# Handing 384 columns of the last row to GpSimd and ScalarE, with the row's pieces cut anew, in a transfer-bound loss kernel

## Chip, cores, metric

One core of a Trainium2 chip. The metric is the device time of one execution in microseconds (us), as the median of several runs. The span in a profile, from the first instruction to the last, is some 1.4 us shorter than the time (82.5 against 83.9).

Row b of a partition is called "row b" below: each of the 128 partitions holds 8 rows of 4096 columns, and a "column" is one fp32 in every partition. VectorE is DVE in the profile, ScalarE is ACT, GpSimd is POOL, SyncE is SP. SBUF and PSUM are the two memories in which the kernel keeps its tiles. A load has landed when its data is there; the releaser of a wait is what ended it.

## The reference

```python
batch, dim = 1024, 4096            # log_input, target: fp32, 16.8 MB each
loss = np.exp(log_input) - target * log_input
return np.mean(loss, axis=-1)      # one number per row
```

## The kernel before

SyncE issues all loads. ScalarE sums exp(x) of a row with its accumulator; VectorE multiplies target by log_input, negated, and sums with its own; a small ScalarE activation joins the two partial sums of a row. The tiles hold six of the eight rows, so rows 6 and 7 go into the space of rows 0 and 3. The last row is loaded in pieces, so that little is left to do once the last piece has landed. Its partial sums stand in columns behind row 3's space of the target tile, against columns of -1 in the log_input tile, so that VectorE's last multiply adds them up as well.

```python
TAIL = [("x", 100), ("t", 52), ("t", 48), ("x", 28), ("t", 14), ("t", 14)]   # last row, in 32 columns
...
loads += [("x", 0, d), ("x", d, 3 * d), ("t", 0, 4 * d)]
for first, rows in ((4, 2), (6, 1)):
    loads += [("x", first * d, rows * d), ("t", first * d, rows * d)]
at = {"x": last_row * d, "t": last_row * d}
for what, w in TAIL:
    loads.append((what, at[what], w * d // 128))
...
    nc.scalar.activation(out=e_dump[:, col : col + w], in_=place("x", lo, w),    # e_dump: PSUM
        func=ACT_F.Exp, bias=0.0, scale=1.0, accum_out=...)
...
    nc.vector.tensor_tensor_reduce(out=place("t", lo, w), in0=place("t", lo, w),
        in1=place("x", lo, w), scale=-1.0, op0=ALU.mult, op1=ALU.add, accum_out=...)
...
    # the last piece: w + n_parts columns, waits for the landing, the last exp
    # and the last-but-one multiply through one semaphore
```

Of the kernel before, what the change touches and what calls it, by code (L numbers as in the profile page):

```python
# [5 lines left out]
ACT_F = mybir.ActivationFunctionType  # L6
ALU = mybir.AluOpType
F32 = mybir.dt.float32


TAIL = [("x", 100), ("t", 52), ("t", 48), ("x", 28), ("t", 14), ("t", 14)]


def before_first_barrier(nc, instructions):





    here, first = nc.cur_bb.bb, nc.main_func.blocks[0]  # L20
    names = {i.name for i in instructions}
    here.instructions = [i for i in here.instructions if i.name not in names]
    at = next(
        k
        for k, i in enumerate(first.instructions)
        if i.engine == mybir.EngineType.SP and i.opcode == "Drain"
    )
    first.instructions = first.instructions[:at] + instructions + first.instructions[at:]


def kernel(tc, log_input, target, out):















    nc = tc.nc
    tc.close()
    tc.compile()  # L49

    P = nc.NUM_PARTITIONS
    n, d = log_input.shape
    nb = n // P
    assert nb * P == n and tuple(target.shape) == (n, d) and nb == 8 and d % 128 == 0
    inv_d = 1.0 / d
    last_row = nb - 1

    x_v = log_input.rearrange("(p b) d -> p (b d)", b=nb)
    t_v = target.rearrange("(p b) d -> p (b d)", b=nb)
    out_v = out.rearrange("(p b) -> p b", b=nb)  # L60


    loads = []
# [6 lines that stand above are left out]
        at[what] += w * d // 128  # L70
    assert at == {"x": nb * d, "t": nb * d}


    def work(kind):
        todo = []
        for i, (what, lo, w) in enumerate(loads):
            if what == kind:
                step = min(w, d)
                todo += [(a, step, i) for a in range(lo, lo + w, step)]
        return todo  # L80

    x_work, t_work = work("x"), work("t")
    n_x, n_t = len(x_work), len(t_work)
    n_parts = n_x - last_row + n_t - last_row - 1

    big = {
        "x": nc.alloc_sbuf_tensor("x_big", [P, 4 * d + n_parts], F32).ap(),
        "t": nc.alloc_sbuf_tensor("t_big", [P, 4 * d + n_parts], F32).ap(),
    }
    mid = {  # L90
        "x": nc.alloc_sbuf_tensor("x_mid", [P, 2 * d], F32).ap(),
        "t": nc.alloc_sbuf_tensor("t_mid", [P, 2 * d], F32).ap(),
    }

    def place(what, lo, w):
        row = lo // d
        if 4 <= row < 6:
            return mid[what][:, lo - 4 * d : lo - 4 * d + w]
        if row >= 6:
            lo -= (6 if row == 6 else 4) * d  # L100
        return big[what][:, lo : lo + w]

    e_dump = nc.alloc_psum_tensor("e_dump", [P, d], F32).ap()

    parts = nc.alloc_sbuf_tensor("parts", [P, 2 * last_row], F32).ap()
    join_dump = nc.alloc_sbuf_tensor("join_dump", [P, 2 * last_row], F32).ap()
    all_loss = nc.alloc_sbuf_tensor("all_loss", [P, nb], F32).ap()

    def part(k):
        return big["t"][:, 4 * d + k : 4 * d + k + 1]  # L110

    landed = [nc.alloc_semaphore(f"landed{i}") for i in range(len(loads) - 1)]


    last_ready = nc.alloc_semaphore("last_ready")
    exp_done = nc.alloc_semaphore("exp_done")
    prod_done = nc.alloc_semaphore("prod_done")
    join_done = nc.alloc_semaphore("join_done")
    ones_done = nc.alloc_semaphore("ones_done")
    loss_done = nc.alloc_semaphore("loss_done")  # L120
    out_done = nc.alloc_semaphore("out_done")


    early = []
    for i, (what, lo, w) in enumerate(loads):
        if what == "x" and lo in (6 * d, 7 * d):
            free = 1 if lo == 6 * d else 4
            nc.sync.wait_ge(exp_done, free)
            nc.sync.wait_ge(prod_done, free)  # L129
        src = x_v if what == "x" else t_v  # L130
        dma = nc.sync.dma_start(out=place(what, lo, w), in_=src[:, lo : lo + w])  # L131
        dma.then_inc(landed[i] if i < len(loads) - 1 else last_ready, 16)
        if lo < 6 * d:
            early.append(dma.ins)
    before_first_barrier(nc, early)


    nc.gpsimd.memset(big["x"][:, 4 * d : 4 * d + n_parts], -1.0).then_inc(ones_done, 1)  # L138


    def join(row, exps):
        nc.scalar.wait_ge(exp_done, exps)
        nc.scalar.activation(  # L143
            out=join_dump[:, 2 * row : 2 * row + 2],
            in_=parts[:, 2 * row : 2 * row + 2],
            func=ACT_F.Copy,
            scale=inv_d,
            accum_out=all_loss[:, row : row + 1],
        ).wait_op(prod_done, row + 1, "sem-ge").then_inc(join_done, 1)

    for k, (lo, w, i) in enumerate(x_work):
        row, col = lo // d, lo % d
        if col == 0 and row >= 2:
            join(row - 2, k)
        elif col == 0 and row == 1:
            nc.scalar.wait_ge(exp_done, k)
        nc.scalar.activation(  # L157
            out=e_dump[:, col : col + w],
            in_=place("x", lo, w),
            func=ACT_F.Exp,  # L160
            bias=0.0,
            scale=1.0,
            accum_out=parts[:, 2 * row : 2 * row + 1] if row < last_row else part(k - last_row),
        ).wait_op(landed[i], 16, "sem-ge").then_inc(
            exp_done if k < n_x - 1 else last_ready, 1
        )
        if col == 0 and row == last_row:
            join(row - 1, k + 1)


    waited = set()
    for j, (lo, w, i) in enumerate(t_work):
        row = lo // d
        x_load = next(ix for a, wx, ix in x_work if a + wx >= lo + w)
        if x_load not in waited:
            nc.vector.wait_ge(landed[x_load], 16)
            waited.add(x_load)
        if j < n_t - 1:
            nc.vector.tensor_tensor_reduce(  # L179
                out=place("t", lo, w),  # L180
                in0=place("t", lo, w),
                in1=place("x", lo, w),
                scale=-1.0,
                scalar=0.0,
                op0=ALU.mult,
                op1=ALU.add,
                accum_out=parts[:, 2 * row + 1 : 2 * row + 2]
                if row < last_row
                else part(n_x - last_row + j - last_row),
            ).wait_op(landed[i], 16, "sem-ge").then_inc(  # L190
                prod_done if j < n_t - 2 else last_ready, 1
            )
        else:
            nc.vector.wait_ge(ones_done, 1)
            nc.vector.wait_ge(exp_done, n_x - 1)
            nc.vector.wait_ge(prod_done, n_t - 2)  # L196
            nc.vector.tensor_tensor_reduce(  # L197
                out=place("t", lo, w + n_parts),
                in0=place("t", lo, w + n_parts),
                in1=place("x", lo, w + n_parts),  # L200
                scale=-inv_d,
                scalar=0.0,
                op0=ALU.mult,
                op1=ALU.add,
                accum_out=all_loss[:, last_row : last_row + 1],
            ).wait_op(last_ready, 18, "sem-ge").then_inc(loss_done, 1)


    nc.sync.wait_ge(join_done, last_row)
    nc.sync.dma_start(out=out_v, in_=all_loss).wait_op(loss_done, 1, "sem-ge").then_inc(  # L210
        out_done, 16
    )
    used = landed + [last_ready, exp_done, prod_done, join_done, ones_done, loss_done]
    nc.sync.sem_clear(range(used[0].num, out_done.num))
    assert all(used[0].num <= s.num < out_done.num for s in used)
    nc.sync.wait_ge(out_done, 16).then_inc(out_done, -16)
# [30 lines left out]
```

## Time and profile before

| | before |
|---|---|
| median of the first three runs | 83.94 us (83.93 to 84.05) |
| bytes loaded | 33.55 MB |
| mean transfer rate over the span | 407 GB/s |
| busy: VectorE / ScalarE / GpSimd | 35.6 / 32.9 / 0.3 us |
| last multiply | 453 columns, 0.63 us |

The engines' busy shares (43%, 40%, 0%) are averages over a long stretch of waiting for data and a short crowded tail. The kernel is bound by its loads (the packets of the load queue took 95.8% of the 16 DMA engines' span, by the page), and what can be changed by compute is only what hangs over their end.

### The profile page before, as it was taken

What the parts mean: (1) busy time and instruction counts of PE and PEld (TensorE: products, weight loads), DVE (VectorE), ACT (ScalarE), POOL (GpSimd) and SP (SyncE); (2) the same over time, 40 slices, a digit from 0 to 9 for tenths busy, and PEclk for the clock granted to TensorE, in tenths of its full rate; (3) what the DMA queues carried; (4) which work ended last, traced back from release to release, by engine and by line L of the source; (5) the groups of instructions that cost most, each with busy time, mean ns of one, the idle gap of its engine ahead of it and who ended that gap; (6) DMA issues with size and microseconds to landing.
All of it is one profiled execution on the core that took longest, in us unless ns stands there. A gap on an engine that the chain in (4) does not pass through costs nothing.

```text
span 82.5 us, 130 instructions
## 1 busy us (share of the span) xinstructions
DVE 35.6 (43%) x22; ACT 32.9 (40%) x33; POOL 0.3 (0%) x5
## 2 busy tenths in 40 slices
DVE  0000000000000000000199999999369995993992
ACT  0325920000592000000000998979792496009450
POOL 0000000000000000000000000000000000000000
DMA  5998998888999990999599799599798999999960
GB/s 127 421 469 381 620 524 381 381 381 381 509 509 509 509 509 0 509 509 509 254 509 445 318 509 509 254 509 509 310 453 381 461 429 410 441 383 420 402 234 2
DMA packets 2017, 33.56 MB, mean 407 GB/s; under 512 B 353, under 2 KB 609, under 8 KB 993
## 3 DMA queue, kind: packets, MB, share of 16 engines
q1 hardware_dynamic: 2016, 33.56, 95.8%
q14 instruction: 1, 0.00, 0.0%
HBM read 33.55 MB, written 0.00 MB: 407 GB/s over the span
## 4 chain that ended last, share of the span: by engine, by line
DMA 69%; DVE 17%; issue 11%; SPq 1%; DVEq 0%
DMA t_big<-in_target_dram 69%; DVE t_big L179 16%; SPq L131 1%; DVE t_big L197 1%; DVE parts L179 0%; DVEq L196 0%; SPq L129 0%; DVE all_loss L197 0%
## 5 line engine op out<-in xcount | busy, mean ns | idle before, releaser
L179 DVE CUSTOM_DVE_ANT_0 t_big<-t_big,x_big 128x4096 f32<-128x4096 f32 (+3 forms) x8 | 26.1, 3298 | 43.4 <-DMA t_big<-in_target_dram 43.4
L157 ACT ACTIVATE e_dump<-x_big 128x4096 f32<-128x4096 f32 (+2 forms) x7 | 21.7, 3095 | 19.6 <-DMA x_big<-in_log_input_dram 19.4
L143 ACT ACTIVATE join_dump<-parts 128x2 f32<-128x2 f32 x7 | 1.4, 203 | 24.3 <-DVE parts L179 24.2
L179 DVE CUSTOM_DVE_ANT_0 t_mid<-t_mid,x_mid 128x4096 f32<-128x4096 f32 x2 | 8.8, 4422 | 2.0 <-DMA t_mid<-in_target_dram 2.0
L157 ACT ACTIVATE e_dump<-x_mid 128x4096 f32<-128x4096 f32 x2 | 7.1, 3568 | 0.0
L157 ACT ACT_TABLE_LOAD x1 | 1.3, 1283 | 3.4 <-PEq L49 3.4
L143 ACT ACTIVATION_READ_ACCUMULATOR join_dump<-parts 128x1 f32 x7 | 1.3, 187 | 0.0
L157 ACT ACTIVATION_READ_ACCUMULATOR e_dump<-x_big 128x1 f32 x7 | 1.3, 186 | 0.0
L197 DVE CUSTOM_DVE_ANT_0 t_big<-t_big,x_big 128x453 f32<-128x453 f32 x1 | 0.6, 631 | 0.0
L179 DVE DVE_READ_ACCUMULATOR2_ANT parts<- 128x1 f32 x7 | 0.6, 81 | 0.0
L157 ACT ACTIVATION_READ_ACCUMULATOR e_dump<-x_mid 128x1 f32 x2 | 0.4, 186 | 0.0
L179 DVE DVE_READ_ACCUMULATOR2_ANT t_big<- 128x1 f32 x3 | 0.2, 81 | 0.0
L138 POOL MEMSET x_big<- 128x5 f32 x1 | 0.1, 103 | 3.0 <-POOLq L49 3.0
L231 POOL MEMSET const-bfloat16-1.0<- 128x1 bf16 x1 | 0.1, 102 | 0.0
L231 POOL MEMSET const-uint8-127<- 128x1 uint8 x1 | 0.1, 102 | 0.0
L231 POOL MEMSET const-float32-0.0<- 128x1 f32 x1 | 0.1, 98 | 0.2 <-issue 0.2
L231 POOL MEMSET const-float32-1.0<- 128x1 f32 x1 | 0.1, 98 | 0.0
L197 DVE DVE_READ_ACCUMULATOR2_ANT all_loss<- 128x1 f32 x1 | 0.1, 81 | 0.0
## 6 DMA issues: line engine op xcount, KB each, us to landing
x_big<-in_log_input_dram SPq DMA_DIRECT2D x1, 6144.0 KB, 21.2
x_big<-in_log_input_dram SPq DMA_DIRECT2D x2, 2048.0 KB, 13.4
x_mid<-in_log_input_dram SPq DMA_DIRECT2D x1, 4096.0 KB, 49.3
t_mid<-in_target_dram SPq DMA_DIRECT2D x1, 4096.0 KB, 58.5
t_big<-in_target_dram SPq DMA_DIRECT2D x1, 2048.0 KB, 24.3
x_big<-in_log_input_dram SPq DMA_DIRECT2D x1, 1600.0 KB, 15.5
t_big<-in_target_dram SPq DMA_DIRECT2D x1, 832.0 KB, 17.1
t_big<-in_target_dram SPq DMA_DIRECT2D x1, 768.0 KB, 18.5
```

The lines of the kernel that those rows point to most:

```text
L131: dma = nc.sync.dma_start(out=place(what, lo, w), in_=src[:, lo : lo + w])
L138: nc.gpsimd.memset(big["x"][:, 4 * d : 4 * d + n_parts], -1.0).then_inc(ones_done, 1)
L143: nc.scalar.activation(out=join_dump[:, 2 * row : 2 * row + 2], in_=parts[:, 2 * row : 2 * row + 2], func=ACT_F.Copy, scale=inv_d, accum_o ...
L157: nc.scalar.activation(out=e_dump[:, col : col + w], in_=place("x", lo, w), func=ACT_F.Exp, bias=0.0, scale=1.0, accum_out=parts[:, 2 * ro ...
L179: nc.vector.tensor_tensor_reduce(out=place("t", lo, w), in0=place("t", lo, w), in1=place("x", lo, w), scale=-1.0, scalar=0.0, op0=ALU.mult ...
L197: nc.vector.tensor_tensor_reduce(out=place("t", lo, w + n_parts), in0=place("t", lo, w + n_parts), in1=place("x", lo, w + n_parts), scale= ...
L231: nc = _bacc.Bacc("TRN2", target_bir_lowering=False, num_devices=1)
```

## The change

Its intent is to take work off VectorE near the end. GpSimd multiplies 384 of the first piece's 2560 columns and ScalarE sums those products. So that VectorE and GpSimd do not get in each other's way in SBUF, ScalarE first copies the other 2176 columns of log_input to PSUM, and VectorE reads them there. The exps of the last row go to an unused part of SBUF, so that they do not write where VectorE reads. The pieces are cut anew.

```diff
-TAIL = [("x", 100), ("t", 52), ("t", 48), ("x", 28), ("t", 14), ("t", 14)]
+TAIL = [("x", 80), ("t", 80), ("x", 30), ("t", 30), ("x", 18), ("t", 8), ("t", 10)]
+SHARE = 12
...
+    gp_x = place("x", shared_lo + dve_w, gp_w)
+    gp_t = place("t", shared_lo + dve_w, gp_w)
+    nc.gpsimd.wait_ge(landed[x_work[last_row][2]], 16)
+    nc.gpsimd.tensor_tensor(out=gp_t, in0=gp_t, in1=gp_x, op=ALU.mult).wait_op(
+        landed[shared_load], 16, "sem-ge").then_inc(gp_done, 1)
...
+        if k == last_row:
+            nc.scalar.activation(
+                out=e_dump[:, :dve_w], in_=place("x", lo, dve_w), func=ACT_F.Copy
+            ).wait_op(landed[i], 16, "sem-ge").then_inc(copy_done, 1)
+        if k == last_row + 1:
+            nc.scalar.activation(out=dump[:, :gp_w], in_=gp_t, func=ACT_F.Copy,
+                scale=-1.0, accum_out=part(n_parts - 1),
+            ).wait_op(gp_done, 1, "sem-ge").then_inc(sum_done, 1)
...
+        x_cols = place("x", lo, w)
+        if j == last_row:
+            w = dve_w
+            x_cols = e_dump[:, :w]
+            nc.vector.wait_ge(copy_done, 1)
...
-                in1=place("x", lo, w),
+                in1=x_cols,
```

(Cut: the semaphores, the place of the exps' output, and one more partial sum.)

More of the change, by code (lines that the diff above doesn't have):

```diff
@@ L83 @@
     n_x, n_t = len(x_work), len(t_work)
-    n_parts = n_x - last_row + n_t - last_row - 1
+    n_parts = n_x - last_row + n_t - last_row
+    shared_lo, shared_w, shared_load = t_work[last_row]
+    gp_w = SHARE * d // 128
+    dve_w = shared_w - gp_w
+    assert shared_lo == x_work[last_row][0] and shared_w <= x_work[last_row][1]
     big = {
@@ L118 @@
     join_done = nc.alloc_semaphore("join_done")
+    copy_done = nc.alloc_semaphore("copy_done")
+    gp_done = nc.alloc_semaphore("gp_done")
+    sum_done = nc.alloc_semaphore("sum_done")
     ones_done = nc.alloc_semaphore("ones_done")
@@ L138 @@
     nc.gpsimd.memset(big["x"][:, 4 * d : 4 * d + n_parts], -1.0).then_inc(ones_done, 1)
+    gp_x = place("x", shared_lo + dve_w, gp_w)
+    gp_t = place("t", shared_lo + dve_w, gp_w)
+    nc.gpsimd.wait_ge(landed[x_work[last_row][2]], 16)
+    nc.gpsimd.tensor_tensor(out=gp_t, in0=gp_t, in1=gp_x, op=ALU.mult).wait_op(
+        landed[shared_load], 16, "sem-ge"
+    ).then_inc(gp_done, 1)
     def join(row, exps):
@@ L149, in join @@
         ).wait_op(prod_done, row + 1, "sem-ge").then_inc(join_done, 1)
+    dump = big["x"][:, d : 2 * d]
     for k, (lo, w, i) in enumerate(x_work):
@@ L156 @@
             nc.scalar.wait_ge(exp_done, k)
+        if k == last_row:
[3 more added lines that the diff above has]
+        if k == last_row + 1:
+            nc.scalar.activation(
+                out=dump[:, :gp_w],
+                in_=gp_t,
+                func=ACT_F.Copy,
+                scale=-1.0,
+                accum_out=part(n_parts - 1),
+            ).wait_op(gp_done, 1, "sem-ge").then_inc(sum_done, 1)
         nc.scalar.activation(
-            out=e_dump[:, col : col + w],
+            out=e_dump[:, col : col + w] if row < last_row else dump[:, col : col + w],
             in_=place("x", lo, w),
@@ L194 @@
             nc.vector.wait_ge(ones_done, 1)
+            nc.vector.wait_ge(sum_done, 1)
             nc.vector.wait_ge(exp_done, n_x - 1)
@@ L212 @@
     )
-    used = landed + [last_ready, exp_done, prod_done, join_done, ones_done, loss_done]
+    used = landed + [last_ready, exp_done, prod_done, join_done, copy_done, gp_done]
+    used += [sum_done, ones_done, loss_done]
     nc.sync.sem_clear(range(used[0].num, out_done.num))
```

## The prediction

(Cut from the prediction: what a PSUM operand costs VectorE, what a column costs GpSimd, who of the two is held, and rival (d), that GpSimd's first multiply comes late. The sum came to -0.04 us, so 83.9 us. Its terms stand, but the last start at 80.45 (the +0.09) holds the cut term for the PSUM operand; without that term the start is the 80.39 of rival (a), and the 0.15 us of slack that ScalarE has up to it shrinks with it. That a PSUM operand speaks against rivals (b) and (c) was not shown then. That GpSimd keeps ahead of ScalarE, and the 85.6 and 84.8 of rivals (b) and (c), rest on a length of its multiply that is cut.)

> **What bounds the kernel now.** I read the page's DMA row first, then the chain of waits, then the timeline of the last microseconds, then the landing times of the single loads.
>
> ```profile
> span 82.5 us, 130 instructions
> ...
> DVE  0000000000000000000199999999369995993992
> ACT  0325920000592000000000998979792496009450
> POOL 0000000000000000000000000000000000000000
> DMA  5998998888999990999599799599798999999960
> ```
>
> The DMA row is at nine tenths in most slices up to the last two. VectorE idles for 41 us, since target arrives late. So the inputs (33.55 MB) set the time, and compute matters only where it hangs over the end of the transfers. The change leaves rows 0 to 6 alone, as the list of instructions per engine confirms. Only the tail can move.
>
> The chain that ended last, in order of time:
>
> ```profile
> 58.92 17.14 DMA t_big<-in_target_dram
> 76.05 0.02 issue
> 76.08 3.05 DVE t_big L179 x3
> ...
> 80.25 0.09 DVE t_big L179
> 80.34 0.02 issue
> 80.36 0.63 DVE t_big L197
> 81.00 0.01 DVE all_loss L197
> ```
>
> From 76.05 on it is no longer a DMA but VectorE that the chain runs through: it works through its backlog of target pieces. The timeline of that stretch:
>
> ```profile
> 74.04 2.84 ACT L157 ACTIVATE e_dump<-x_big 128x3200 f32<-128x3200 f32 x1 [4.51 <-DMA x_big<-in_log_input_dram]
> 76.08 1.89 DVE L179 CUSTOM_DVE_ANT_0 t_big<-t_big,x_big 128x1664 f32<-128x1664 f32 x1 [1.44 <-DMA t_big<-in_target_dram]
> 77.96 1.76 DVE L179 CUSTOM_DVE_ANT_0 t_big<-t_big,x_big 128x1536 f32<-128x1536 f32 x1
> 79.10 0.92 ACT L157 ACTIVATE e_dump<-x_big 128x896 f32<-128x896 f32 x1 [1.72 <-DMA x_big<-in_log_input_dram]
> 79.70 0.62 DVE L179 CUSTOM_DVE_ANT_0 t_big<-t_big,x_big 128x448 f32<-128x448 f32 x1
> 80.36 0.63 DVE L197 CUSTOM_DVE_ANT_0 t_big<-t_big,x_big 128x453 f32<-128x453 f32 x1
> 81.03 0.35 SPq L210 DMA_DIRECT2D out_dram<-all_loss  x1
> ```
>
> The view of one line's DMA issues gives each load's time from issue to landing. Issue start plus that time: log_input's 3200 columns land at 58.55 + 15.5 = 74.05, its 896 at 59.88 + 19.2 = 79.08, target's last two pieces at 60.36 + 19.3 = 79.66 and 60.86 + 19.4 = 80.26; row 6 of target landed at 45.88 + 24.3 = 70.18. So the last piece of data is there at 80.26 and the last multiply starts at 80.36. VectorE's backlog over the transfers is therefore only 0.1 us. What lies behind the last landing is 0.1 of backlog, 0.63 for the last multiply, 0.03, and 1.4 for the output's transfer. Only the first two, about 0.7 us of 83.94, are in reach of this change.
>
> [...]
>
> **Working scales, from rows of the trace.** VectorE: 4422 ns for 4096 columns and 624 for 448 give 1.041 ns a column plus 158 ns. ScalarE exp: 3580 for 4096 and 922 for 896 give 0.831 ns a column plus 178; an accumulator read starts 0.05 to 0.07 before an activation's end, takes 0.19, and the next ScalarE instruction starts 0.09 after the read starts. Transfers: 3200 columns in 74.05 - 70.18 = 3.87 us and 448 in 0.59 give 1.19 ns a column and about 0.05 us for each load.
>
> **The change part by part.**
> *Loads.* The same 8192 columns in seven loads in place of six: 0.05 us more. Working forward from 70.18: log_input 2560 at 73.3, target 2560 at 76.4, log_input 960 at 77.6, target 960 at 78.8, log_input 576 at 79.5, target 256 at 79.9, target 320 at 80.3. All issues stand ready by about 61.5 (six of them are over at 61.3 now, each some 0.45 us), long before the data, so the extra issue is hidden.
>
> *VectorE.* Its first piece now has 2560 - 384 = 2176 columns: 2.42 us from 76.4[...]: free at 78.85 or so. The 960 columns landed at 78.8: 1.16 us, to 80.0. The 256 columns landed at 79.9: 0.42, to 80.42. The last one can start at about 80.45, in place of 80.36. It has 320 + 7 = 327 columns in place of 453: 0.50 in place of 0.63. End at 80.95 against 80.99: a gain of 0.04. Without giving 384 columns away, the same sizes would put VectorE 384 x 1.041 = 0.40 us later[...]. In both kernels VectorE waits for the last row's first target piece; that one now lands 0.3 us later (76.4 against 76.06) and leaves 384 columns less to do, so the two nearly cancel.
>
> *ScalarE.* It was idle from 69.5 to 74.04, and now has a copy and a sum more. Copy of 2176: 73.3 to 75.2 (1.81 + 0.1), ahead of the target's landing at 76.4, so it costs VectorE no wait. Exp 2560: 75.2, its accumulator read at 77.45 to 77.65. Join of row 6: 77.74, next instruction at 77.94. Sum of the 384 products: 77.94 to 78.46 for the next start. Exp 960: 78.46, next at 79.46. Exp 576: landed 79.5, accumulator read out at 80.3. That is just ahead of VectorE's 80.45, and 0.15 us is all its slack.
>
> *GpSimd.* Multiply of 384 columns from 76.4[...]. ScalarE asks for it at 77.94[...].
>
> *Sum.* Transfers +0.05, which VectorE's lag covers; VectorE's last start +0.09; last multiply -0.13. Total -0.04 us, with an uncertainty of 0.1 from all these small terms. I choose 83.9 us, which is level.
>
> **The rivals.**
> (a) *Everything fits and VectorE has no backlog.* If the PSUM read costs nothing extra, the last start is at 80.39, set by VectorE, or 80.31 by the last landing, and the gain is 0.1 to 0.17: 83.8. Nothing could give more, as the last 320 columns can't start before they land.[...]
> (b) *GpSimd becomes the wait.* If the multiply is held until VectorE's 2176 columns are through, at 78.85[...]; sum, exp 960 and exp 576 follow on ScalarE, 0.52 + 1.0 + 0.85 later, so that the last multiply starts at 82.2: 1.8 later, minus 0.13, 85.6 us, at the edge of 2%.[...] A slower multiply, of 2.5 us say, would give 84.7.
> (c) *VectorE is held by GpSimd*[...]: 84.8.[...]
> [...]
>
> **Range and chances.** The main case and (a) hold 83.75 to 84.0 and carry about four fifths. A small slip of ScalarE or GpSimd (some tenths) makes up most of the rest, up to 84.5. (b), (c) and (d) carry about a tenth, of which some 5 points are over 2%. A gain of 2% (1.68 us) is out of reach: less than 0.8 us lies behind the last landing ahead of the output. So 83.9, from 83.7 to 84.5; faster 0.01, within 2% 0.94, slower 0.05.
>
> **What the profile after would show.** Right: target's last landing at 80.2 to 80.4; the 2176-column piece at 2.4 to 2.5 us, starting with its landing at 76.4; the GpSimd multiply starting there too and over before 78, with no idle time of ScalarE ahead of its sum; the last VectorE piece at 0.50 us from 80.3 to 80.5. Wrong: ScalarE idle with GpSimd named as releaser (b); the 2176-column piece at over 3 us (c)[...]. The prediction fails if the GpSimd multiply takes over 2 us, or if the added instructions move something ahead of 70 us.

## The result

The changed kernel takes 83.98 us (83.77 to 84.14, 6 runs), the one before 83.97 us (83.82 to 84.05, 6 runs). Ratios here and below are those from the runs of both kernels in the same rounds; they are not quite the ratio of the medians quoted. Here the ratio is 1.0001, with a 95% interval of 0.9982 to 1.002: the same.

The page of the changed kernel, busy tenths in 40 slices (each about 2.06 us), for the two engines that gained work, and DMA:

```profile
span 82.5 us, 141 instructions
ACT  0324930000493000000000998979792496049990
POOL 0000000000000000000000000000000000000400
DMA  6999998888999982999599899699699999999960
```

ScalarE, half idle before in the last four slices (9450), is now full there (9990). GpSimd has one visible stretch. DMA is as full as before, to the same slice.

The chain of waits of the changed kernel, in order of time (start, length, what; "issue" is time in which the profile shows no wait):

```profile
59.05 17.43 DMA t_big<-in_target_dram
76.48 0.02 issue
76.50 1.23 DVE t_big L222
77.73 1.12 issue
78.85 0.86 DVE t_big L222 x2
...
80.50 0.02 issue
80.53 0.50 DVE t_big L241
```

It is the same chain: transfers, then VectorE's pieces up to the last multiply. Neither GpSimd nor ScalarE is in it. The timeline of its tail (start, length, engine, line, operation; in brackets idle time and what ended it):

```profile
70.32 4.43 DVE L222 CUSTOM_DVE_ANT_0 t_big<-t_big,x_big 128x4096 f32<-128x4096 f32 x1 [1.00 <-DMA t_big<-in_target_dram]
73.41 1.99 ACT L184 ACTIVATE e_dump<-x_big 128x2176 f32<-128x2176 f32 x1 [3.76 <-DMA x_big<-in_log_input_dram]
76.50 2.42 DVE L222 CUSTOM_DVE_ANT_0 t_big<-t_big,e_dump 128x2176 f32<-128x2176 f32 x1 [1.75 <-DMA t_big<-in_target_dram]
76.55 1.00 POOL L160 TENSOR_TENSOR t_big<-t_big,x_big 128x384 f32<-128x384 f32 x1 [73.00 <-DMA t_big<-in_target_dram]
78.04 0.51 ACT L188 ACTIVATE x_big<-t_big 128x384 f32<-128x384 f32 x1
78.85 0.08 DVE L222 DVE_READ_ACCUMULATOR2_ANT t_big<- 128x1 f32 x1
78.92 1.16 DVE L222 CUSTOM_DVE_ANT_0 t_big<-t_big,x_big 128x960 f32<-128x960 f32 x1
79.68 0.68 ACT L195 ACTIVATE x_big<-x_big 128x576 f32<-128x576 f32 x1
80.00 0.08 DVE L222 DVE_READ_ACCUMULATOR2_ANT t_big<- 128x1 f32 x1
80.06 0.43 DVE L222 CUSTOM_DVE_ANT_0 t_big<-t_big,x_big 128x256 f32<-128x256 f32 x1
80.53 0.50 DVE L241 CUSTOM_DVE_ANT_0 t_big<-t_big,x_big 128x327 f32<-128x327 f32 x1
```

GpSimd's multiply is over at 77.55, before ScalarE asks for it at 78.04. The last piece was issued at about 61.5 and took 18.9 to land, so it was there at 80.4; the last multiply began 0.1 later, just as before.

**A measure that the scatter of the runs does not blur.** Runs of one kernel differ by 0.2 to 0.4 us (83.82 to 84.05 and 83.77 to 84.14 above). Part of that is when the stream of loads reaches row 7, which neither kernel changes (row 6's multiply starts at 70.21 and 70.43 in two traces of the kernel before). So for every trace I take the *tail*: from the start of VectorE's row 6 piece, which starts with the landing of row 6, to the end of the last multiply. Before it is 80.36 + 0.63 - 70.21 = 10.78 us; in the changed kernel 80.53 + 0.50 - 70.32 = 10.71.

### The profile page after: what moved, and what is told of

It is laid out like the page before. It is cut to its first block, busy times and chain, and to the rows that moved or that the text cites. A ratio compares the mean times of both kernels' runs of the same rounds, so it can differ in the third digit from the quotient of the medians.

```text
span 82.5 us, 141 instructions
## 1 busy us (share of the span) xinstructions
DVE 35.2 (43%) x22; ACT 35.5 (43%) x38; POOL 1.3 (2%) x6
## 4 chain that ended last, share of the span: by engine, by line
DMA 70%; DVE 15%; issue 12%; SPq 1%; DVEq 0%
DMA t_big<-in_target_dram 70%; DVE t_big L222 15%; SPq L147 1%; DVE t_big L241 1%; DVE parts L222 0%; DVEq L240 0%; SPq L145 0%; DVE all_loss L241 0%
## 5 line engine op out<-in xcount | busy, mean ns | idle before, releaser
L222 DVE CUSTOM_DVE_ANT_0 t_big<-t_big,x_big 128x4096 f32<-128x4096 f32 (+2 forms) x7 | 23.5, 3386 | 42.1 <-DMA t_big<-in_target_dram 42.1
L195 ACT ACTIVATE e_dump<-x_big 128x4096 f32<-128x4096 f32 x5 | 17.9, 3580 | 13.4 <-DMA x_big<-in_log_input_dram 13.3
L195 ACT ACTIVATE x_big<-x_big 128x2560 f32<-128x2560 f32 (+2 forms) x3 | 4.0, 1330 | 0.1
L184 ACT ACTIVATE e_dump<-x_big 128x2176 f32<-128x2176 f32 x1 | 2.0, 1988 | 3.8 <-DMA x_big<-in_log_input_dram 3.8
L222 DVE CUSTOM_DVE_ANT_0 t_big<-t_big,e_dump 128x2176 f32<-128x2176 f32 x1 | 2.4, 2421 | 1.7 <-DMA t_big<-in_target_dram 1.7
L160 POOL TENSOR_TENSOR t_big<-t_big,x_big 128x384 f32<-128x384 f32 x1 | 1.0, 1000 | 73.0 <-DMA t_big<-in_target_dram 73.0
L195 ACT ACTIVATION_READ_ACCUMULATOR x_big<-x_big 128x1 f32 x3 | 0.6, 186 | 0.0
L241 DVE CUSTOM_DVE_ANT_0 t_big<-t_big,x_big 128x327 f32<-128x327 f32 x1 | 0.5, 499 | 0.0
L188 ACT ACTIVATE x_big<-t_big 128x384 f32<-128x384 f32 x1 | 0.5, 507 | 0.0
```

The source lines that it names most:

```text
L160: nc.gpsimd.tensor_tensor(out=gp_t, in0=gp_t, in1=gp_x, op=ALU.mult).wait_op(landed[shared_load], 16, "sem-ge").then_inc(gp_done, 1)
L184: nc.scalar.activation(out=e_dump[:, :dve_w], in_=place("x", lo, dve_w), func=ACT_F.Copy).wait_op(landed[i], 16, "sem-ge").then_inc(copy_d ...
L188: nc.scalar.activation(out=dump[:, :gp_w], in_=gp_t, func=ACT_F.Copy, scale=-1.0, accum_out=part(n_parts - 1),).wait_op(gp_done, 1, "sem-g ...
L195: nc.scalar.activation(out=e_dump[:, col : col + w] if row < last_row else dump[:, col : col + w], in_=place("x", lo, w), func=ACT_F.Exp, ...
L241: nc.vector.tensor_tensor_reduce(out=place("t", lo, w + n_parts), in0=place("t", lo, w + n_parts), in1=place("x", lo, w + n_parts), scale= ...
```

## The experiments

My theory after the prediction: the change is level because two things that would each move the end nearly cancel, and nearly every piece of VectorE's work is held by a landing anyway. Rivals: the transfers alone set the end, and neither part matters; or work taken off VectorE counts in full, and something else gave it back.

| run | edit | median us | ratio to before (95%) | tail us |
|---|---|---|---|---|
| before (its profile) | | 83.97 | 1 | 10.78 |
| e9_before_again | none | 84.06 | 1.0008 (0.9994 to 1.0023) | 10.81 |
| changed (its profile) | | 83.98 | 1.0001 (0.9982 to 1.002) | 10.71 |
| e1_after_again | none | 84.04 | 1.0006 (0.9983 to 1.0029) | 10.71 |
| e2_sizes_only | no share, no copy | 84.18 | 1.0028 (1.0004 to 1.0052) | 11.29, late loads |
| e12_sizes_only_again | the same | 84.17 | 1.0033 (1.002 to 1.0046) | 10.99 |
| e3_share_only | sizes of before | 84.01 | 1.0016 (0.9989 to 1.0043) | 10.81 |
| e10_psum_only | no share, copy kept | 84.11 (one run) | | 10.95 |
| e4_no_psum | share, no copy | 85.39 | 1.0184 (1.015 to 1.0217) | 12.30 |
| e5_share24 | 768 columns | 84.42 | 1.0059 (1.0036 to 1.0082) | 11.18 |
| e6_share40 | 1280 columns | 85.95 | 1.0231 (1.0214 to 1.0248) | 12.69 |
| e7_trim | a try at more | 84.27 | 1.0027 (1.0013 to 1.0041) | 10.98 |
| e8_gpsimd_alone | two early multiplies on GpSimd | 83.84 (one run) | | 10.70 |
| e11_gpsimd_two_tiles | three early multiplies on GpSimd | 83.85 (one run) | | 10.70 |

### The same kernels again

> The changed kernel unaltered, as the yardstick for the three beside it. Theory (several small terms cancel: transfers later by 0.07 us, VectorE's last start later by 0.17, its last multiply shorter by 0.13): 83.9 to 84.05 us, within 0.1% of the kernel before, last landing near 80.4, last multiply of 0.50 us from about 80.5. Rival (the tail's compute does not matter, the transfers alone set the end): the same time; this run does not tell them apart, the next two do.

It came as expected: 84.04 us, tail 80.50 + 0.50 - 70.29 = 10.71.

> The kernel before, unaltered, for a second trace of it and for what two equal kernels differ by. In its one trace row 6 of target landed at 70.19, in the changed kernel's traces at 70.26 to 70.30, before anything changed. If that is the scatter of the transfers, the second trace of before has it anywhere from 70.1 to 70.4 and the end of VectorE's work 10.8 us after it; if the changed kernel does delay something early, the second trace has 70.2 again. Ratio within 0.2% of one.

The second trace of the kernel before:

```profile
70.43 4.42 DVE L179 CUSTOM_DVE_ANT_0 t_big<-t_big,x_big 128x4096 f32<-128x4096 f32 x1 [1.01 <-DMA t_big<-in_target_dram]
79.94 0.62 DVE L179 CUSTOM_DVE_ANT_0 t_big<-t_big,x_big 128x448 f32<-128x448 f32 x1
80.61 0.63 DVE L197 CUSTOM_DVE_ANT_0 t_big<-t_big,x_big 128x453 f32<-128x453 f32 x1
```

Row 6 starts at 70.43, later than in the changed kernel's traces, so the start is scatter. The tail is 10.81. Two traces of before have 10.78 and 10.81, two of the changed kernel 10.71 and 10.71 (and 10.70 in e8 and e11, whose tails are unaltered): the change shortens the tail by 0.09 us, a thousandth of the time, which the timed runs can't show (two equal kernels came out 1.0008 apart here).

### The sizes alone

```diff
-SHARE = 12
+SHARE = 0
-    (GpSimd's multiply, ScalarE's copy and sum, and the wait for them)
-            x_cols = e_dump[:, :w]
```

> The new piece sizes without GpSimd's share, its sum and the PSUM copy: VectorE multiplies all 2560 columns of the first piece from SBUF. Theory: VectorE is 384 x 1.04 = 0.40 us later at every piece from 76.5 on: 960 columns from about 79.3, 256 from 80.45, the last from 80.95, end of its work 81.45 in place of 81.03, so 84.4 us, 0.4 us or 0.5% over the changed kernel. Rival (transfers alone set the end): level with the changed kernel, within 0.1 us.

The time was 84.18, so 0.14 over the changed kernel and not clear of it (intervals 1.0004 to 1.0052 and 0.9983 to 1.0029). Its profile fell on late transfers: row 7's first piece of log_input set ScalarE going 3.42 us after row 6's multiply had started (73.81 - 70.39) in place of 3.09, so its tail of 11.29 is not compared. Hence once more:

> The sizes alone once more, as the first time its profile fell on late transfers and its time was not clear of the changed kernel's. From that trace: the last multiply starts 0.39 us after the last landing in place of 0.11, so 0.28 us over the changed kernel and, with before 0.07 above the changed kernel by their traces, 0.2 us or 0.25% over before: ratio 1.0025. By the first theory (0.40 us): 1.004. By the rival that only the transfers count: 1.000.

```profile
70.36 4.42 DVE L201 CUSTOM_DVE_ANT_0 t_big<-t_big,x_big 128x4096 f32<-128x4096 f32 x1 [1.01 <-DMA t_big<-in_target_dram]
76.56 2.83 DVE L201 CUSTOM_DVE_ANT_0 t_big<-t_big,x_big 128x2560 f32<-128x2560 f32 x1 [1.76 <-DMA t_big<-in_target_dram]
79.31 1.15 DVE L201 CUSTOM_DVE_ANT_0 t_big<-t_big,x_big 128x960 f32<-128x960 f32 x1
80.39 0.42 DVE L201 CUSTOM_DVE_ANT_0 t_big<-t_big,x_big 128x256 f32<-128x256 f32 x1
80.85 0.50 DVE L219 CUSTOM_DVE_ANT_0 t_big<-t_big,x_big 128x326 f32<-128x326 f32 x1
```

The ratio 1.0033 excludes one (and 1.0006, which the one load more would be worth by the prediction's 0.05 us), so the rival of transfers alone falls. Its interval holds both 1.0025 and 1.004, so it is the trace that decides between these. The tail is 80.85 + 0.50 - 70.36 = 10.99, which is 0.28 over the changed kernel, not the 0.40 that I first expected. Two short waits took the difference. With its data there, a piece starts together with the accumulator read of the one ahead, 0.08 before that one is over (79.31 against 76.56 + 2.83 = 79.39), and in this run the 960 and the 256 columns do so. In the changed kernel the 960 columns start only at 78.92, although the read of the 2176 begins at 78.85, and the 256 columns at 80.06, with the read of the 960 at 80.00: VectorE waits there for landings, 0.07 and 0.06. So of the 0.40 us that GpSimd takes off, 0.28 reaches the end.

### The share alone

```diff
-TAIL = [("x", 80), ("t", 80), ("x", 30), ("t", 30), ("x", 18), ("t", 8), ("t", 10)]
+TAIL = [("x", 100), ("t", 52), ("t", 48), ("x", 28), ("t", 14), ("t", 14)]
```

> The piece sizes of before with GpSimd's share, the sum and the PSUM copy: VectorE's first piece has 1280 columns in place of 1664. Theory: the next piece, 1536 columns, lands at 77.93 and keeps VectorE busy to 79.7 as before, so the 0.4 us taken off ahead of it turns into idle time before it (77.55 to 77.93): level with the kernel before, within 0.1 us, last multiply again from about 80.35. A rival that counts work taken off VectorE as won: 0.4 us faster, 83.55.

It was level, 1.0016 with one in the interval, and the tail is 80.96 + 0.63 - 70.78 = 10.81, as before (10.78 and 10.81). Where the 0.4 us went stands in brackets:

```profile
76.67 1.49 DVE L222 CUSTOM_DVE_ANT_0 t_big<-t_big,e_dump 128x1280 f32<-128x1280 f32 x1 [1.46 <-DMA t_big<-in_target_dram]
78.56 1.76 DVE L222 CUSTOM_DVE_ANT_0 t_big<-t_big,x_big 128x1536 f32<-128x1536 f32 x1 [0.39 <-DMA t_big<-in_target_dram]
80.29 0.62 DVE L222 CUSTOM_DVE_ANT_0 t_big<-t_big,x_big 128x448 f32<-128x448 f32 x1
```

The 384 columns (0.40 us) became 0.39 us of idle time ahead of the next landing. The rival that counts them as won falls. Alone, then, the share gives nothing, and the sizes cost about 0.2 us (10.99 against 10.78 and 10.81). Together they give 0.09: the new sizes make the last multiply smaller, and the share pays for what they would cost.

The traces say more closely where the 0.09 comes from. In both kernels the last-but-one multiply of target starts with the landing of its own piece, some 0.05 after VectorE is free. Counted from row 6's multiply it starts at 9.49 and 9.51 in the two traces of before and at 9.51 here, with 384 columns fewer ahead of it; in the changed kernel at 9.74 (80.06 - 70.32), in e5, with twice the share, at 9.72. From there to the end it is 1.29 us before (80.99 - 79.70) and 0.97 in the changed kernel (81.03 - 80.06). So the new sizes bring that landing 0.24 later and make what follows it 0.32 shorter. The share's part is only that VectorE is free by then: in e12 it is not, and the piece starts at 10.03.

### Without the PSUM copy

```diff
-        if k == last_row:
-            nc.scalar.activation(out=e_dump[:, :dve_w], ..., func=ACT_F.Copy)
-            x_cols = e_dump[:, :w]
+            x_cols = place("x", lo, w)
```

(Cut: VectorE's wait for the copy.)

> The changed kernel without the PSUM copy: VectorE reads both inputs of its 2176 columns from SBUF while GpSimd multiplies its 384. If two SBUF inputs hold GpSimd off altogether: GpSimd starts or goes on only at about 78.9, ends near 79.9, ScalarE's sum and two exps follow, last multiply from about 82.3, 85.7 us, with ScalarE idle ahead of its sum and GpSimd as the releaser. If instead VectorE is held by GpSimd: its 2176-column piece takes some 3.4 us in place of 2.42 and the time is 84.9. If there is no contention: level, 83.9 to 84.05, with 1.00 us for GpSimd and 2.42 for VectorE, and the copy is not needed.

```profile
76.45 2.42 DVE L217 CUSTOM_DVE_ANT_0 t_big<-t_big,x_big 128x2176 f32<-128x2176 f32 x1 [1.75 <-DMA t_big<-in_target_dram]
76.49 3.23 POOL L160 TENSOR_TENSOR t_big<-t_big,x_big 128x384 f32<-128x384 f32 x1 [72.92 <-DMA t_big<-in_target_dram]
78.86 1.88 DVE L217 CUSTOM_DVE_ANT_0 t_big<-t_big,x_big 128x960 f32<-128x960 f32 x1
79.76 0.52 ACT L184 ACTIVATE x_big<-t_big 128x384 f32<-128x384 f32 x1 [3.60 <-POOL t_big L160]
82.06 0.50 DVE L236 CUSTOM_DVE_ANT_0 t_big<-t_big,x_big 128x327 f32<-128x327 f32 x1 [0.96 <-ACT x_big L191]
```

This is rival (b) of the prediction, made to happen: 85.39 us, with ScalarE idle for 3.60 us and GpSimd as the releaser. VectorE came first by 0.04 us and was not slowed (2.42). GpSimd took 3.23 in place of 1.00 and ended at 79.72, 0.85 after VectorE's piece. In turn VectorE's next piece, with two SBUF inputs and GpSimd now under way, took 1.88 in place of 1.16. So without the copy the share costs some 1.35 us (85.39 against 84.04), though in the changed kernel nothing waits for the copy (over at 75.40, with VectorE's piece starting at 76.50).

### Larger shares

```diff
-SHARE = 12
+SHARE = 24        # e6: 40
```

> Twice the share: GpSimd 768 columns, VectorE 1792 of the first piece, sizes of pieces as in the changed kernel. Theory (VectorE already waits for its landings after the first piece, and ScalarE has no slack): VectorE's first piece 2.02 us, then idle until 78.9, nothing gained[...]; ScalarE's sum starts at 78.45 and is 0.32 us longer, its last exp ends 0.5 later, so the last multiply starts from about 81.05 with ScalarE as the releaser: 84.5 us, 0.5 over the changed kernel. Rival (VectorE's load is what counts, more taken off is more won): 0.1 us faster or more.

```profile
76.66 1.81 POOL L160 TENSOR_TENSOR t_big<-t_big,x_big 128x768 f32<-128x768 f32 x1 [73.13 <-DMA t_big<-in_target_dram]
79.03 1.16 DVE L222 CUSTOM_DVE_ANT_0 t_big<-t_big,x_big 128x960 f32<-128x960 f32 x1 [0.39 <-DMA t_big<-in_target_dram]
81.12 0.50 DVE L241 CUSTOM_DVE_ANT_0 t_big<-t_big,x_big 128x327 f32<-128x327 f32 x1 [0.53 <-ACT x_big L195]
```

The 0.40 us more that were taken off VectorE are idle time again (0.39), and the last multiply now waits for ScalarE. 84.42 us against 84.5 expected.

> GpSimd multiplies 1280 columns, so that it is still at work[...] when VectorE's 960 columns with two SBUF inputs start at 78.9, after its 1280 from PSUM. Who is held? If the second to start is held until the first is done[...]: VectorE's 960 take 1.75 us in place of 1.16[...]. If VectorE has the right of way: [...]the 960 columns 1.16. If they share: both longer, by some tenths. ScalarE's sum waits for GpSimd in any case: last multiply from about 82.6, 86.0 us, or about 87.1 where GpSimd is held.

```profile
76.83 2.89 POOL L160 TENSOR_TENSOR t_big<-t_big,x_big 128x1280 f32<-128x1280 f32 x1 [73.29 <-DMA t_big<-in_target_dram]
79.20 1.53 DVE L222 CUSTOM_DVE_ANT_0 t_big<-t_big,x_big 128x960 f32<-128x960 f32 x1 [0.92 <-DMA t_big<-in_target_dram]
```

85.95 us against 86.0. GpSimd, first here, took what it takes without a neighbour (2.89 us, against 2.88 in e11 below); VectorE, second, took 0.37 longer. The two overlap for 76.83 + 2.89 - 79.20 = 0.52 us. In e4 VectorE's 960 columns overlapped with GpSimd for 79.72 - 78.86 = 0.86 and took 0.72 longer. GpSimd, second in e4, overlapped with VectorE's 2176 columns for 76.45 + 2.42 - 76.49 = 2.38 and took 2.23 longer. So in these three overlaps, each with two SBUF inputs on VectorE, the second to start, whichever it was, lost the time of the overlap but for some 0.15 us (0.15, 0.14 and 0.15), as if held until the first was done. Where the 0.15 comes from, no run shows.

### What GpSimd and PSUM cost by themselves

> The changed kernel with two multiplies more on GpSimd near the start, 384 and 2048 columns of a tile of its own, while VectorE stands idle. If VectorE's PSUM operand keeps it off GpSimd's reads altogether: the 384 columns alone take 1.00 us, as beside VectorE's 2176.[...] The 2048 columns give the price of a column[...]. Time level with the changed kernel.

```profile
L162 POOL TENSOR_TENSOR probe<-probe 128x2048 f32<-128x2048 f32 x1 | 3.6, 3600 | 0.1
L162 POOL TENSOR_TENSOR probe<-probe 128x384 f32<-128x384 f32 x1 | 0.8, 827 | 0.1
```

The 384 columns took 0.827 us there, 2048 took 3.600: the 384 took less than the 1.00 beside VectorE. But both inputs were one tile, so VectorE was not yet to blame:

> The multiplies of GpSimd alone again, with VectorE idle, but with two different tiles as inputs, as in the real one, at 384, 768 and 1280 columns. Alone with one tile as both inputs 384 columns took 0.83 us and a column 1.67 ns; beside VectorE's PSUM piece 1.00 us and 2.11 ns. If it is the second tile that costs: 1.00, 1.81 and 2.89 us, as beside VectorE. If it is VectorE: 0.83, 1.47 and 2.32 us.

The groups of instructions of that run (busy us, mean ns of one):

```profile
L164 POOL TENSOR_TENSOR probe_a<-probe_a,probe_b 128x1280 f32<-128x1280 f32 x1 | 2.9, 2880 | 0.1
L164 POOL TENSOR_TENSOR probe_a<-probe_a,probe_b 128x768 f32<-128x768 f32 x1 | 1.8, 1803 | 0.1
L164 POOL TENSOR_TENSOR probe_a<-probe_a,probe_b 128x384 f32<-128x384 f32 x1 | 1.0, 993 | 0.1
```

With two tiles and VectorE idle it is 993, 1803 and 2880 ns; beside VectorE's PSUM piece it was 1000, 1810 and 2890 (the last also beside 0.52 us of the 960 columns). So VectorE with one input in PSUM costs GpSimd nothing that shows (about 10 ns, and the profile's times of GpSimd are rough), and it is the second tile that makes a column 2.1 ns in place of 1.67: (2880 - 993) / 896 against (3600 - 827) / 1664. Why a second tile costs, no run shows.

(Cut: the first branch, by which the PSUM operand makes both times longer. "If not" is: if it costs VectorE nothing.)

> Sizes as in the changed kernel, no GpSimd share, but the copy: VectorE reads its whole first piece, 2560 columns, from the PSUM copy. In the run of sizes alone, from SBUF, that piece lasted 2.83 us and the next one, with its data there, started 2.75 us after it.[...] If not: 2.83 and 2.75[...].

VectorE's first two pieces in that run:

```profile
76.49 2.82 DVE L206 CUSTOM_DVE_ANT_0 t_big<-t_big,e_dump 128x2560 f32<-128x2560 f32 x1 [1.74 <-DMA t_big<-in_target_dram]
79.23 1.15 DVE L206 CUSTOM_DVE_ANT_0 t_big<-t_big,x_big 128x960 f32<-128x960 f32 x1
```

2.82 us and 2.74 to the next piece's start, against 2.83 and 2.75 from SBUF. The PSUM operand costs VectorE nothing here.

### A try at a faster version

```diff
-TAIL = [("x", 80), ("t", 80), ("x", 30), ("t", 30), ("x", 18), ("t", 8), ("t", 10)]
-SHARE = 12
+TAIL = [("x", 84), ("t", 84), ("x", 28), ("t", 28), ("x", 16), ("t", 7), ("t", 9)]
+SHARE = 20
-    loads += [("x", 0, d), ("x", d, 3 * d), ("t", 0, 4 * d)]
+    loads += [("x", 0, 4 * d), ("t", 0, 4 * d)]
(the join of row 6 moved ahead of the last row's first exp; the sum's output, of no use, to another place)
```

> A version that the last runs point to: one load fewer at the start, last-row pieces of 84, 28 and 16 with the last target piece cut 7 and 9, GpSimd 640 columns, and the join of row 6 ahead of the last row's first exp, which saves ScalarE a wait on itself. Theory: VectorE's lag behind the last landing goes from 0.11 to 0.08, the last multiply from 0.50 to 0.47, one load less is 0.05 us: 0.1 to 0.15 us faster than the changed kernel, which five rounds can hardly tell from level. If GpSimd's 640 columns[...] or ScalarE come late, it is level or slower, with ScalarE as the releaser of the last multiply.

It is slower than the kernel before by 0.27%, 84.27 us, tail 10.98. The last multiply waited 0.32 us for ScalarE. The chain of waits of that run says why:

```profile
77.00 1.55 POOL t_big L160
78.55 0.02 issue
78.57 0.83 ACT x_big L189 x2
79.40 1.55 ACT x_big L196 x4
80.95 0.02 issue
80.98 0.47 DVE t_big L240
```

GpSimd's 640 columns, ScalarE's sum and its last two exps have become one chain with no gap from 77.00 to the end. This is the second branch of what was expected. This one try, of four edits at once, gave no version faster than either kernel.

## Why the prediction was right

**The bound.** Right: the transfers set the time, and the tail is all that moved.

**Transfers, 0.05 later for one load more.** Right. From row 6's landing to that of the last piece it is 10.05 to 10.08 us in the three traces with the sizes of before, and 10.12 to 10.14 in the four with the changed kernel's tail: 0.07. (The packed traces hold landings to the nanosecond; the views round the time to landing to 0.1 us.)

**VectorE.** The last multiply was put at 80.45 and came at 80.53, with everything 0.11 later than the prediction's clock (row 6's multiply at 70.32, not 70.21). Counted from that multiply it started 10.21 in and not 10.15 as before: 0.06 later, where 0.09 was predicted. It lasts 0.50 in place of 0.63, as predicted. The sum is a gain of 0.07 by these two traces and 0.09 by the four, where 0.04 was predicted; the timed runs are level.

Here there is luck in the number, as the path was not the predicted one. Of VectorE in the trace before the prediction says "it works through its backlog of target pieces", and its sum lets VectorE run from 76.4 to the end without a wait for data. But before, the multiplies of 1664, 1536 and 448 columns each start 0.02 after their own landing (76.05, 77.93 and 79.67); only the last one waits for VectorE itself. In the changed kernel VectorE's three pieces ahead of the last multiply followed each other faster than summed, by 0.24 in all (the term for the PSUM operand, cut above, is part of it). Two waits for landings (0.07 and 0.06) and a longer step to the last multiply (0.12 where 0.03 was allowed) took 0.22 back, so the stretch from VectorE's first piece to the last multiply came out at 4.03 against 4.05.

**The PSUM term**, cut above. Wrong: e10 shows no cost (2.82 us for 2560 columns against 2.83 from SBUF). It did not matter, as the 960 columns had to wait 0.07 us for their landing.

**"Without giving 384 columns away, the same sizes would put VectorE 384 x 1.041 = 0.40 us later."** The mechanism is right, the size is not: 0.28 by e12. The 0.40 takes VectorE as busy without a break in both, and leaves out the 0.13 that it waits for landings in the changed kernel.

**ScalarE.** The sum was put at 77.94 and came at 78.04, the last exp at 79.5 and came at 79.68, about the 0.11 of the clock and a little more. That it has next to no slack was right (its last accumulator read is over at 80.46, the last multiply starts at 80.53), and e5 and e7 ran into it: there the last multiply waited 0.53 and 0.32 us for ScalarE.

**GpSimd.** It took 1.00 us and was done at 77.55, and ScalarE asked for it at 78.04: 0.49 us of slack.

**The rivals.** (a) was nearest, as PSUM costs VectorE nothing that shows in e10. (b) is real and was averted by the copy alone, the only edit in e4: 85.6 predicted for it, 85.39 measured in e4. (c) too happens, in e4 and e6, where GpSimd is under way first and VectorE has two SBUF inputs: its 960 columns took 1.88 and 1.53 us in place of 1.16. (d), cut above, did not happen: the changed kernel's one multiply started 0.05 us after VectorE's piece (76.55 against 76.50) and took 1.00 us, and in e11 the first multiply took 993 ns at about 6 us and the last, of as many columns, 1004 ns.

## What to carry to other kernels

In the tail of this transfer-bound kernel, work taken off an engine was worth only what that engine lagged behind the next landing: of 0.40 us taken off VectorE, 0.28 reached the end with the new sizes (e12 against the changed kernel) and nothing with the old ones (e3, 0.39 us idle). So look for idle time before a landing between its pieces before you move work away. VectorE's waits of 0.07 and 0.06 us stood in no bracket of the timeline: compare a piece's start with the accumulator read of the one ahead, or the wait passes for a backlog, as it did here. Choose piece sizes and the share together, as here neither helps without the other (tails of 10.99 and 10.81 us alone, 10.71 together, 10.78 and 10.81 before), and stop when the helper engine (here ScalarE, with 84.42 us in e5 and 84.27 in e7) has no slack left. To run GpSimd beside a VectorE multiply with both inputs in SBUF, take one of the two out of it; without that the share cost 1.35 us here (e4).
